# Attention on one core: dividing outputs instead of probabilities, and splitting a pair's heads through DRAM

## The chip, the cores and the metric

The kernel runs on one core of a Trainium2 chip. The time is that of one launch in device microseconds. Three runs are given for the kernel before.

## The reference

A decoder trunk of two layers works on 1040 tokens (16 learned meta tokens and 1024 real ones) with 1024 features. Layer 0 is a gated linear recurrence with a feed-forward block, layer 1 is causal attention with a forget gate and a feed-forward block. The change lies in the attention of layer 1, which has 16 heads of 64 features:

```
q = (x @ w_q) per head;  k, v = rmsnorm(h) @ kv_w per head;  c = cumsum(log_sigmoid(zf))
logits = q @ k.T * 64**-0.5 + (c[query] - c[key]),  causal
p = softmax(logits)
o = p @ v;   mix = o @ w_out
```

All arithmetic is float32 in the reference.

## The kernel before

Features lie on partitions and tokens along the free dimension. A float32 product is made of three matmuls on float32r parts: each operand is split into a high part (a rounding cast on ACT) and a low part (operand minus high part, a subtraction on DVE). `split` at line 98 (with the cast at line 97) does that for weights and for activations.

Heads are handled in pairs, eight pairs of 128 partitions. `project` (line 784) multiplies the normalised activations by the pair's weights for k, v or q in three token blocks (`BLK_A`, or `BLK_B` for q) and writes the product, times the normaliser r2, to a whole unit of SBUF: unit 17 for k, 18 for q, 16 for v (lines 798 and 800). `turn` (line 803) transposes v. `halves` (line 826) makes the operands of one head out of its 64 partitions of the pair's unit: the keys `ks` hold the high part on one half of the partitions and the low part on the other, and two query tiles `qs` hold high and low parts in both arrangements. That is four casts on ACT (lines 837, 841, 842, 844) and two subtractions on DVE (lines 838, 843) for each head and block. One matmul over 128 partitions then sums two products of parts. The tile `cn` holds the forget sums of the head, broadcast from DRAM (line 835).

The work is cut into 48 units: 16 heads by three groups of 342 queries. `score_steps` makes a unit's probabilities in three strips of 114 queries (QT): score matmuls (lines 879 to 882), an addition of c with a running minimum on DVE (line 884), the exponential with its sum on ACT (line 887), the reciprocal of the sum (line 888) and the multiplication of the whole strip by it on DVE (line 889). `sum_steps` transposes the strips on PE (line 909), splits the transposes into `pTh` on ACT (line 913) and `pTl` on DVE (line 914), sums over keys in one PSUM bank `po` (lines 921, 922), and adds the two halves of the bank to the head's output (line 933 on ACT, 934 on DVE), which is stored to DRAM `ob` (line 936). The last pair's outputs stay in SBUF.

PE's order is written out by hand. `scores_ahead` runs the sums of unit s beside the scores of unit s + 1 and calls `halves` for unit s + 2; `dense` is a second stream with the projections of pairs 1 to 7 and the first half of the output projection (`one`); `weave` mixes the two by their matmul columns. Pair 0 is projected before, in `heads0`. On the other engines and on SP's DMA queue, a scheduler orders instructions by readiness and priority; every queue runs in that order. The output projection loads the stored outputs in `oload` (line 990) into units that the projections' activations held, and splits them into `oh` and `ol`.

Of the kernel before, what the change touches and what calls it, by code (L numbers as in the profile page):

```python
# [8 lines left out]
F32 = mybir.dt.float32  # L9
F32R = mybir.dt.float32r  # L10
# [8 lines left out]
P = 128  # L19
# [36 lines left out]
def tile_yoco(ctx: ExitStack, tc: tile.TileContext, hT, gains, lbl, w_in, head_g, w_oa,  # L56
# [14 lines left out]
    def unit(i, name, dt=F32):  # L71
        return ar.tile([P, D if i in (30, 31) else T], dt, tag=f"u{i}", name=nm(name))
# [4 lines left out]
    def tmp(tag, n, dt=F32):  # L77
        return sm.tile([P, 358], dt, tag=tag, name=nm(tag), bufs=SMB[tag])[:, :n]

    def f(ap):  # L80
        return ap.bitcast(F32)
# [201 lines left out]
    h_dram = [nc.dram_tensor(f"h{j}", [KT, P, T], F32, kind="Internal").ap() for j in range(3)]  # L283
    o_dram = nc.dram_tensor("ob", [KT, P, T], F32, kind="Internal").ap()
    c_dram = nc.dram_tensor("csum", [BH, T], F32, kind="Internal").ap()


    hn = [(unit(kt, f"hnh{kt}", F32R), unit(8 + kt, f"hnl{kt}", F32R)) for kt in range(KT)]
# [470 lines left out]

    KS, QS, VS, CN = [24, 25], [(33, 34), (6, 7)], [[35, 36], [4, 5]], [12, 13]
    PU = [14, 15, 39, 44, 38, 19]
    NB = len(BLK_B)
# [5 lines left out]
    pair = [dict() for _ in range(KT)]  # L770
    head_ = [dict() for _ in range(2 * KT)]
    seen = set()
    count = {"p": 0, "pt": 0}

    def rot(key, slots):
# [8 lines left out]
    def project(which, hp, i):  # L784

        p = pair[hp]
        if which not in p:
            src, c0, g, u = {"k": (kv_w, 0, 8, 17), "v": (kv_w, D, 8, 16), "q": (w_q, 0, 4, 18)}[which]
            p[which] = (WA.cols(src, [c0 + hp * P], gsb[:, g]), unit(u, which))
        w, dst = p[which]  # L790
        t0, n = (BLK_B if which == "q" else BLK_A)[i]
        pt, sl = psum("pj")[:, :n], slice(t0, t0 + n)
        yield from mm3s(pt, [(w(kt), y[kt]) for kt in range(KT)], sl)
        while hp and which != "v" and ("split", 2 * hp - 1, i) not in seen:
            yield None
        with tc.high_priority(offset=OFF):
            if which == "q":
                V.scalar_tensor_tensor(dst[:, sl], pt, -HD ** -0.5, r2[:, sl], ALU.mult, ALU.mult)
            else:
                V.tensor_mul(dst[:, sl], pt, r2[:, sl])  # L800
        seen.add((which, hp, i))

    def turn(hp, i):

        p = pair[hp]
        if i == 0:
            p["vs"] = [unit(VS[hp % 2][j], f"vs{j}", F32R)[:, :D].rearrange("p (k c) -> p k c", c=P) for j in range(2)]
            p["tail"] = tmp("res", 2 * P, F32R).rearrange("p (k c) -> p k c", c=P)
        vT = p["v"][1]
        pt = psum("g")  # L810
        for j, (k0, kw) in enumerate(KEYS[3 * i:3 * i + 3]):
            PE.transpose(pt[:kw, j * P:(j + 1) * P], vT[:, k0:k0 + kw], ident)
        p3 = pt.rearrange("p (k c) -> p k c", c=HD)
        n = 3 - i // 2
        for j in range(2):
            parts = [(p["vs"][j][:QT, 3 * i:3 * i + n], p3[:QT, j:2 * n:2])]
            if i == 0:
                parts.append((p["vs"][j][96:, :1], p3[96:, j:j + 1]))
            elif i == 2:
                parts.append((p["tail"][:QT, j:j + 1], p3[:QT, 4 + j:5 + j]))  # L820
            for d, q in parts:
                A.copy(d[:, :, :HD], q)
                V.tensor_sub(d[:, :, HD:], q, f(d[:, :, :HD]))
        seen.add(("turn", hp, i))

    def halves(n, i):

        h = head_[n]
        if i == 0:
            h["k"] = unit(KS[n % 2], "ks", F32R)  # L830
            h["q"] = [unit(u, "qs", F32R) for u in QS[n % 2]]
            h["c"] = unit(CN[n % 2], "cn")
        a, b = (hi, lo) if n % 2 else (lo, hi)
        sl = slice(BLK_A[i][0], BLK_A[i][0] + BLK_A[i][1])
        nc.sync.dma_start(h["c"][:, sl], c_dram[n:n + 1, sl].to_broadcast([P, BLK_A[i][1]]))
        x, k = pair[n // 2]["k"][1], h["k"]
        A.copy(k[a, sl], x[a, sl])
        V.tensor_sub(k[b, sl], x[a, sl], f(k[a, sl]))
        sl = slice(BLK_B[i][0], BLK_B[i][0] + BLK_B[i][1])
        x, (q1, q2) = pair[n // 2]["q"][1], h["q"]  # L840
        A.copy(q1[a, sl], x[a, sl])
        A.copy(q2[b, sl], x[a, sl])
        V.tensor_sub(q2[a, sl], x[a, sl], f(q1[a, sl]))
        A.copy(q1[b, sl], f(q2[a, sl]))
        seen.add(("split", n, i))

    def dense():
        for hp in range(1, KT):
            for i in range(NB):
                yield from project("v", hp, i)  # L850
                if i:
                    turn(hp, i - 1)
                    yield 6 * P
            for i in range(NB):
                yield from project("k", hp, i)
                if i == 0:
                    turn(hp, 2)
                    yield 6 * P
                yield from project("q", hp, i)
        while ("split", 2 * KT - 1, NB - 1) not in seen:  # L860
            yield None
        yield from one()

    def score_steps(s):


        n, g = divmod(s, NB)
        h, g0 = head_[n], BLK_B[g][0]
        out = h[g] = []
        for i in range(3):  # L870
            q0 = g0 + i * QT
            kn = q0 + QT
            L = unit(rot("p", PU), "L")
            c4 = sm.tile([P, 8], F32, tag="c4", name=nm("c4"), bufs=4)[:QT]
            pcs = pieces(kn)
            for x, (a, b) in enumerate(pcs):
                pt = psum("pd")[:QT, :b - a]
                last = x == len(pcs) - 1
                PE.matmul(pt, h["q"][0][:, q0:q0 + QT], h["k"][:, a:b], start=True, stop=False)  # L879
                PE.matmul(pt, h["q"][1][:, q0:q0 + QT], h["k"][:, a:b], start=False, stop=not last)  # L880
                if last:
                    PE.matmul(pt[:, b - a - QT:], identb[:QT], maskb[:QT], start=False, stop=True)
                with tc.high_priority(offset=OFF):
                    V.tensor_tensor_reduce(L[:QT, a:b], pt, h["c"][:QT, a:b], 1.0, 3e38 if x == 0 else c4[:, x - 1:x],
                                           ALU.add, ALU.min, c4[:, x:x + 1])
                if last:
                    A.activation(L[:QT, :kn], L[:QT, :kn], AF.Exp, scale=-1.0, bias=c4[:, x:x + 1], accum_out=c4[:, 5:6])
                    V.reciprocal(c4[:, 6:7], c4[:, 5:6])
                    V.tensor_scalar(L[:QT, :kn], L[:QT, :kn], c4[:, 6:7], None, ALU.mult)  # L889
                    out.append((L, kn))  # L890
                yield 2 * (b - a) + last * QT

    def sum_steps(s):

        n, g = divmod(s, NB)
        g0, gn = BLK_B[g]
        pu = head_[n][g]
        p, j = pair[n // 2], n % 2
        nk = 3 * g + 3
        av = psum("po")  # L900
        pT = {}

        def turned(kt):
            c0 = rot("pt", [0, gn, 2 * gn])
            k0, kw = KEYS[kt]
            f0 = max(0, kt - 3 * g)
            pt = psum("g")
            for i in range(f0, 3):
                PE.transpose(pt[:kw, i * QT:(i + 1) * QT], pu[i][0][:QT, k0:k0 + kw], ident[:QT, :QT])  # L909
            ts = slice(f0 * QT, gn)  # L910
            th, tl = pTh[:kw, c0:c0 + gn], pTl[:kw, c0:c0 + gn]
            with tc.high_priority(offset=OFF):
                A.copy(th[:, ts], pt[:kw, ts])
                V.tensor_sub(tl[:, ts], pt[:kw, ts], f(th[:, ts]))  # L914
            pT[kt] = th, tl, ts
            return 2 * (gn - f0 * QT)

        def summed(kt):
            th, tl, ts = pT[kt]
            v = (p["vs"][j][:, kt] if kt < 8 else p["tail"][:, j])[:th.shape[0]]  # L920
            PE.matmul(av[:, ts], v, th[:, ts], start=(kt == 0), stop=False)  # L921
            PE.matmul(av[:, ts], v, tl[:, ts], start=False, stop=(kt == nk - 1))  # L922
            return 2 * (gn - ts.start)

        for kt in range(nk + AHEAD):
            if kt < nk:
                yield turned(kt)
            if kt >= AHEAD:
                yield summed(kt - AHEAD)
        r, r_ = (hi, lo) if j else (lo, hi)  # L930
        hp, sl = n // 2, slice(g0, g0 + gn)
        ot = o_last[0][:, sl] if hp == KT - 1 else tmp("sq", gn)
        A.copy(ot[r], av[r, :gn])
        V.tensor_add(ot[r], ot[r], av[r_, :gn])
        if hp < KT - 1:
            nc.sync.dma_start(o_dram[hp][r, sl], ot[r])

    def scores_ahead():

# [136 lines left out]
```

## Time and profile before

| | |
|---|---|
| median of three runs | 2875.55 us (2873.24 to 2882.78) |
| profiled execution, its time | 2883.05 us |
| its span | 2881.1 us |
| mean granted TensorE clock | 0.982 |
| busy share: PE, PEld, DVE, ACT, POOL | 96%, 94%, 64%, 44%, 13% |
| share of the DMA engines' span, hardware queue | 19.2% |

PE is the matmul engine and PEld its weight loads, DVE is VectorE, ACT ScalarE, POOL GpSimd, SP the engine that issues the DMAs. A line L889 is line 889 of the kernel before. The span runs from the first to the last instruction. A granted clock of 1.00 is 2.4 GHz and 0.50 is 1.2 GHz; a value between is a mean over both. In rows of waits, the engine and line on the left stood still until the one on the right was done.

### The profile page before, as it was taken

Reading aid. Unit: us, or ns where it says so; the run is one execution under the profiler, and the core shown is the slowest. Engines: PE = TensorE matmul, PEld = TensorE weight load, DVE = VectorE, ACT = ScalarE, POOL = GpSimd, SP = SyncE. Lnnn points to the kernel's source line nnn. Section 1 sums busy time; section 2 is a strip of 40 time slices with the busy share of each in tenths; the row PEclk is TensorE's granted clock in tenths of the full one; section 3 lists DMA queues with packets and bytes.
Section 4 is the critical chain, followed back from the end, with each engine's and each line's share of the span. In section 5 each row is a group of like instructions: output and inputs, shape, how many; then the busy total and the mean of one; then the engine's idle time right before and its main releaser. Section 6 shows DMA issues by size and latency. Waiting matters only on the chain. (4 is left out here: it accounts for less than half of the span.)

```text
span 2881.1 us, 45581 instructions
## 1 busy us (share of the span) xinstructions
PE 2768.6 (96%) x17706; PEld 2709.2 (94%) x17706; DVE 1830.8 (64%) x3737; ACT 1258.2 (44%) x2421; POOL 369.6 (13%) x741
## 2 busy tenths in 40 slices
PE   8999999989999999999889999999989999999997
PEld 8999999989999999999789988898989999999997
DVE  5545445285655655566878888887684665565566
ACT  6445445455322322233566666666555232232232
POOL 2000000041100000004400000000240100010012
PEclk9999999999999999999899999999999999999999
DMA  4111111142211111112311111112242111121103
GB/s 132 30 38 30 38 40 49 37 125 62 66 38 52 45 52 38 44 52 67 92 45 45 45 45 45 45 45 93 70 124 59 45 52 52 30 65 39 52 30 113
DMA packets 202921, 163.14 MB, mean 57 GB/s; under 512 B 13984, under 2 KB 194128, under 8 KB 202704
## 3 DMA queue, kind: packets, MB, share of 16 engines
q1 hardware_dynamic: 202704, 160.23, 19.2%
q8 instruction: 138, 2.26, 0.3%
q14 instruction: 79, 0.65, 0.1%
HBM read 139.53 MB, written 20.66 MB: 56 GB/s over the span
## 5 line engine op out<-in xcount | busy, mean ns | idle before, releaser
L145 PE MATMUL pj<-x,wh 128*128 128x342 f32 (+1 forms) x2640 | 871.1, 330 | 12.6 <-DVE u L607 6.3
L149 PE MATMUL pj<-x,wl 128*128 128x342 f32 (+1 forms) x2640 | 849.3, 322 | 2.8 <-DVE wl L98 2.8
L148 PE MATMUL pj<-x,wh 128*128 128x342 f32 (+1 forms) x2640 | 849.3, 322 | 0.0
L145 PEld LDWEIGHTS pj<-x,wh 128*128 128x128 f32 x2640 | 500.8, 190 | 18.9 <-DVE u L607 7.2
L149 PEld LDWEIGHTS pj<-x,wl 128*128 128x128 f32 x2640 | 499.9, 189 | 3.1 <-DVE wl L98 3.1
L148 PEld LDWEIGHTS pj<-x,wh 128*128 128x128 f32 x2640 | 501.5, 190 | 0.1
L145 PE MATMUL g<-h,wh 128*128 128x342 f32 (+1 forms) x1056 | 339.0, 323 | 0.3
L149 PE MATMUL g<-h,wl 128*128 128x342 f32 (+1 forms) x1056 | 337.7, 321 | 0.4 <-DVE wl L138 0.4
L148 PE MATMUL g<-h,wh 128*128 128x342 f32 (+1 forms) x1008 | 323.8, 322 | 0.0
L97 ACT CAST wh<-raw 128x1024 fp32r<-128x1024 f32 x142 | 146.0, 1045 | 341.6 <-PE g L148 282.1
L145 PE MATMUL pj<-hnh,wh 128*128 128x356 f32 (+1 forms) x720 | 261.8, 364 | 9.3 <-ACT wh L97 7.0
L681 DVE TENSOR_TENSOR acc<-acc,g 128x342 f32<-128x342 f32 (+1 forms) x288 | 147.2, 511 | 193.6 <-PE g L149 193.4
L98 DVE TENSOR_TENSOR wl<-raw,wh 128x1024 fp32r<-128x1024 f32 x142 | 180.6, 1281 | 87.1 <-ACT wh L97 76.3
L149 PE MATMUL pj<-hnh,wl 128*128 128x356 f32 (+1 forms) x720 | 233.1, 324 | 0.8 <-DVE wl L98 0.8
L148 PE MATMUL pj<-hnl,wh 128*128 128x356 f32 (+1 forms) x720 | 232.8, 323 | 0.0
L612 ACT ACTIVATE y<-u,cw 128x342 f32<-128x342 f32 (+1 forms) x258 | 150.5, 584 | 182.6 <-DVE u L607 171.9
L188 POOL TENSOR_TENSOR acc<-acc,sq 128x342 f32<-128x342 f32 (+1 forms) x162 | 168.9, 1049 | 426.5 <-ACT sq L187 396.4
L613 DVE SCALAR_TENSOR_TENSOR y<-u,cw,y 128x342 f32<-128x342 f32 (+1 forms) x258 | 148.5, 576 | 111.4 <-ACT y L612 111.2
L607 DVE TENSOR_TENSOR u<-pj,r 128x342 f32<-128x342 f32 (+1 forms) x258 | 132.2, 513 | 114.1 <-PE pj L149 110.8
L145 PEld LDWEIGHTS g<-h,wh 128*128 128x128 f32 x1056 | 198.7, 189 | 2.5 <-ACT h L97 0.6
L149 PEld LDWEIGHTS g<-h,wl 128*128 128x128 f32 x1056 | 199.4, 189 | 0.6 <-DVE wl L138 0.6
L148 PEld LDWEIGHTS g<-h,wh 128*128 128x128 f32 x1008 | 190.6, 189 | 0.7 <-DVE h L98 0.2
(237 smaller groups left out, 4937.8 us busy)
## 6 DMA issues: line engine op xcount, KB each, us to landing
raw<-in_w_up_dram SPq DMA_DIRECT2D x84, 512.0 KB, 4.0
raw<-in_w_dn_dram SPq DMA_DIRECT2D x42, 512.0 KB, 4.7
raw<-in_w_in_dram SPq DMA_DIRECT2D x32, 512.0 KB, 4.1
raw<-in_kv_w_dram SPq DMA_DIRECT2D x16, 512.0 KB, 4.1
res<-h SPq DMA_DIRECT2D x44, 171.0 KB, 2.8
h<-mix SPq DMA_DIRECT2D x40, 171.0 KB, 2.2
cn<-csum SPq DMA_DIRECT2D x32, 171.0 KB, 3.6
raw<-in_w_oa_dram SPq DMA_DIRECT2D x8, 512.0 KB, 3.5
```

What stands on the lines that cost most here:

```text
L97: A.copy(hi, src)
L98: V.tensor_sub(lo, src, f(hi))
L145: PE.matmul(pt, wh, xh[:, sl], start=(j == 0), stop=False)
L148: PE.matmul(pt, wh, xl[:, sl], start=False, stop=False)
L149: PE.matmul(pt, wl, xh[:, sl], start=False, stop=(j == n - 1))
L188: eng.tensor_add(acc, acc, sq)
L607: V.tensor_mul(u[:, 2:], pt, r()[:, sl])
L612: A.activation(y, u[:, 2:], AF.Copy, scale=cw[:, j, 2:3])
L613: V.scalar_tensor_tensor(y, u[:, 1:n + 1], cw[:, j, 1:2], y, ALU.mult, ALU.add)
L681: V.tensor_add(acc_u[ot][:, sl], acc_u[ot][:, sl], pt)
```

## The change

1. The probabilities are no longer divided by their sums. The reciprocals of a unit's three strips go to a small tile `rg` and by a DMA of 4-byte pieces to DRAM (`rsum`). At the beginning of the unit's sums they are loaded again, broadcast over 64 partitions, into `rr` (tag `rstd`), and the output is multiplied by them.
2. A unit's output is put together in another way: two copies on ACT out of `po` (lines 955, 956), an addition and a multiplication on POOL (lines 957, 958). For the last pair the addition stays on DVE, and a multiplication is added there (lines 951, 952).
3. The store of an output to `ob` is issued at the beginning of the next unit's sums, behind the load of its `rr`.
4. k and q of a pair are split as a whole, one cast and one subtraction over 128 partitions for each block, into two units (17, 18) that all pairs share. Both parts are stored to DRAM (`kq`), and `halves` loads a head's partitions into both halves of its tiles: two loads for the keys and four for the queries for each block.
5. The dense stream projects k, then q, then v of a pair, where it projected v and then k and q in turn. It does not wait any more for the previous pair's heads to be split. The v transposes of a block come behind the projection that follows.

```diff
+    r_dram = nc.dram_tensor("rsum", [BH, T], F32, kind="Internal").ap()
+    kq_dram = nc.dram_tensor("kq", [2, KT, 2, P, T], F32, kind="Internal").ap()
...
         if which not in p:
-            src, c0, g, u = {"k": (kv_w, 0, 8, 17), "v": (kv_w, D, 8, 16), "q": (w_q, 0, 4, 18)}[which]
-            p[which] = (WA.cols(src, [c0 + hp * P], gsb[:, g]), unit(u, which))
+            src, c0, g = {"k": (kv_w, 0, 8), "v": (kv_w, D, 8), "q": (w_q, 0, 4)}[which]
+            p[which] = (WA.cols(src, [c0 + hp * P], gsb[:, g]), unit(16, "v") if which == "v" else kq_dram["kq".index(which), hp])
...
-        while hp and which != "v" and ("split", 2 * hp - 1, i) not in seen:
-            yield None
         with tc.high_priority(offset=OFF):
-            if which == "q":
-                V.scalar_tensor_tensor(dst[:, sl], pt, -HD ** -0.5, r2[:, sl], ALU.mult, ALU.mult)
+            if which == "v":
+                V.tensor_mul(dst[:, sl], pt, r2[:, sl])
             else:
-                V.tensor_mul(dst[:, sl], pt, r2[:, sl])
+                if not kq_parts:
+                    kq_parts.extend(unit(u, "kq", F32R) for u in (17, 18))
+                x, xh, xl = tmp("u", n), *(u[:, sl] for u in kq_parts)
+                if which == "q":
+                    V.scalar_tensor_tensor(x, pt, -HD ** -0.5, r2[:, sl], ALU.mult, ALU.mult)
+                else:
+                    V.tensor_mul(x, pt, r2[:, sl])
+                split(xh, xl, x)
+                for j, part in enumerate((xh, xl)):
+                    nc.sync.dma_start(dst[j][:, sl], f(part))
...
-        a, b = (hi, lo) if n % 2 else (lo, hi)
+        r = (lo, hi)[n % 2]
         sl = slice(BLK_A[i][0], BLK_A[i][0] + BLK_A[i][1])
+        for j, rows in enumerate((lo, hi)):
+            nc.sync.dma_start(f(h["k"][rows, sl]), kq_dram[0, n // 2, j][r, sl])
         nc.sync.dma_start(h["c"][:, sl], c_dram[n:n + 1, sl].to_broadcast([P, BLK_A[i][1]]))
-        x, k = pair[n // 2]["k"][1], h["k"]
-        A.copy(k[a, sl], x[a, sl])
-        V.tensor_sub(k[b, sl], x[a, sl], f(k[a, sl]))
         sl = slice(BLK_B[i][0], BLK_B[i][0] + BLK_B[i][1])
-        x, (q1, q2) = pair[n // 2]["q"][1], h["q"]
-        A.copy(q1[a, sl], x[a, sl])
-        A.copy(q2[b, sl], x[a, sl])
-        V.tensor_sub(q2[a, sl], x[a, sl], f(q1[a, sl]))
-        A.copy(q1[b, sl], f(q2[a, sl]))
+        for x, q in enumerate(h["q"]):
+            for j, rows in enumerate((lo, hi)):
+                nc.sync.dma_start(f(q[rows, sl]), kq_dram[1, n // 2, j ^ x][r, sl])
...
     def dense():
+        todo = []
         for hp in range(1, KT):
-            for i in range(NB):
-                yield from project("v", hp, i)
-                if i:
-                    turn(hp, i - 1)
-                    yield 6 * P
-            for i in range(NB):
-                yield from project("k", hp, i)
-                if i == 0:
-                    turn(hp, 2)
-                    yield 6 * P
-                yield from project("q", hp, i)
+            for which in "kqv":
+                for i in range(NB):
+                    yield from project(which, hp, i)
+                    if todo:
+                        turn(*todo.pop())
+                        yield 6 * P
+                    if which == "v":
+                        todo.append((hp, i))
+        turn(*todo.pop())
...
-                    V.reciprocal(c4[:, 6:7], c4[:, 5:6])
-                    V.tensor_scalar(L[:QT, :kn], L[:QT, :kn], c4[:, 6:7], None, ALU.mult)
+                    V.reciprocal(rg[:, i:i + 1], c4[:, 5:6])
+                    if i == 2:
+                        nc.sync.dma_start(r_dram[n, g0:g0 + 3 * QT].rearrange("(i q) -> q i", q=QT), rg)
...
+        rr = tmp("rstd", gn)
+        rows = r if hp == KT - 1 else lo
+        nc.sync.dma_start(rr[rows], r_dram[n:n + 1, sl].to_broadcast([HD, gn]))
+        for dst, src in stores:
+            nc.sync.dma_start(dst, src)
+        stores.clear()
...
-        ot = o_last[0][:, sl] if hp == KT - 1 else tmp("sq", gn)
-        A.copy(ot[r], av[r, :gn])
-        V.tensor_add(ot[r], ot[r], av[r_, :gn])
-        if hp < KT - 1:
-            nc.sync.dma_start(o_dram[hp][r, sl], ot[r])
+        if hp == KT - 1:
+            ot = o_last[0][:, sl]
+            A.copy(ot[r], av[r, :gn])
+            V.tensor_add(ot[r], ot[r], av[r_, :gn])
+            V.tensor_mul(ot[r], ot[r], rr[r])
+        else:
+            ot, o2 = tmp("sq", gn)[lo], tmp("sq2", gn)[lo]
+            A.copy(ot, av[lo, :gn])
+            A.copy(o2, av[hi, :gn])
+            G.tensor_add(ot, ot, o2)
+            G.tensor_mul(ot, ot, rr[lo])
+            stores.append((o_dram[hp][r, sl], ot))
```

How the instructions move is shown at two places. The first is DVE in the loop's regular part, before the change (an ISA row is the addition with minimum and the read of its result):

```order
L888 RECIPROCAL c_2116_15539<-c_2116_15539 114x1
L843 TENSOR_TENSOR qs_15613<-q_15467,qs_15612 64x342
L889 TENSOR_SCALAR L_15538<-L_15538,c_2116_15539 114x584
L888 RECIPROCAL c_2123_15570<-c_2123_15570 114x1
L889 TENSOR_SCALAR L_15569<-L_15569,c_2123_15570 114x698
L934 TENSOR_TENSOR sq_15595<-sq_15595,po_15518 64x342
L800 TENSOR_TENSOR k_15331<-pj_15545,r_829_6125 128x342
L914 TENSOR_TENSOR pTl_13244<-g_15623,pTh_13243 128x342
L884 ISA L_15634,c_2135_15635<-pd_15636,cn_15161 114x406
L884 ISA c_2135_15635 114x1
L838 TENSOR_TENSOR ks_15611<-k_15331,ks_15611 64x342
```

And DVE in the regular part with the change:

```order
L893 ISA L_15540,c_2151_15541<-pd_15542,cn_15301 114x356
L893 ISA c_2151_15541 114x1
L807 SCALAR_TENSOR_TENSOR u_15563<-pj_15462,r_829_6125 128x342
L897 RECIPROCAL rg_15492<-c_2151_15541 114x1
L932 TENSOR_TENSOR pTl_13274<-g_15555,pTh_13273 114x342
L98 TENSOR_TENSOR kq_12767<-u_15563,kq_12766 128x342
L932 TENSOR_TENSOR pTl_13274<-g_15573,pTh_13273 114x342
```

Between the subtractions for `pTl` there is no multiplication of a strip, no head's subtraction and no output addition; one subtraction for the pair's block (L98) has come.

The second place is SP's DMA queue, before the change, over some two and a half heads' units:

```order
L936 DMA ob<-sq_14266 64x342
L835 DMA cn_14740<-csum 128x356
L835 DMA cn_14740<-csum 128x342 x2
L936 DMA ob<-sq_14431 64x342
L115 DMA raw_15324<-in_kv_w_dram 128x8x128
L936 DMA ob<-sq_14621 64x342
L936 DMA ob<-sq_14721 64x342
L835 DMA cn_15161<-csum 128x356
```

With the change, in a part of one unit, where a second head of a pair is loaded:

```order
L848 DMA ks_15298<-kq 64x356 x2
L849 DMA cn_15301<-csum 128x356
L853 DMA qs_15299<-kq 64x342
L899 DMA rsum<-rg_14858 114x3x1
L853 DMA qs_15300<-kq 64x342 x2
L848 DMA ks_15298<-kq 64x342 x2
L849 DMA cn_15301<-csum 128x342
L916 DMA rstd_15000<-rsum 64x342
L918 DMA ob<-sq_14974 64x342
```

The loads of a head's parts, the store and the load of the reciprocals and the store of an output of the unit before share the queue, and the head's loads stand around the reciprocals' store.

## Rows read from the trace of the kernel before

**Rows 1.** The page, busy us of each engine (share of the span) and instructions.

```profile
PE 2768.6 (96%) x17706; PEld 2709.2 (94%) x17706; DVE 1830.8 (64%) x3737; ACT 1258.2 (44%) x2421; POOL 369.6 (13%) x741
```

**Rows 2.** Stretches: busy us of PE, PEld, DVE, ACT, POOL; clock, DMA share, GB/s.

```profile
1345.00:1470.00 125.00, 103.21 (x571) 96.61 (x570) 98.61 (x201) 69.68 (x152) 48.92 (x41) 0.85 0.31 91
1470.00:1950.00 480.00, 459.42 (x3101) 434.01 (x3100) 406.39 (x1143) 302.90 (x756) 32.26 (x17) 0.99 0.16 44
1950.00:1980.00 30.00, 22.98 (x124) 19.67 (x123) 25.40 (x51) 23.94 (x48) 0.00 (x0) 0.78 0.55 170
1980.00:2080.00 100.00, 99.42 (x668) 97.14 (x668) 62.04 (x159) 55.81 (x122) 8.85 (x10) 1.00 0.17 54
1740.00:1750.00 10.00, 7.40 (x36) 6.21 (x36) 8.72 (x19) 5.16 (x14) 1.90 (x1) 0.83 0.11 33
1890.00:1900.00 10.00, 8.42 (x45) 7.83 (x44) 7.23 (x15) 6.44 (x15) 1.78 (x1) 0.83 0.20 59
```

**Rows 3.** Waits of PE, 1470 to 1950 us: total us, times, longest us.

```profile
PE po L922 <- DVE pTl L914: 10.6, 15, 2.2
PE g L909 <- DVE pTl L914: 2.7, 4, 0.9
PE g L909 <- DVE L L889: 1.7, 2, 0.9
PE po L921 <- ACT pTh L913: 1.6, 4, 0.7
```

**Rows 4.** Groups by line on DVE, 1470 to 1950 us: busy us, mean ns, idle before.

```profile
L889 DVE TENSOR_SCALAR L<-L,c 114x698 f32<-114x698 f32 (+8 forms) x119 | 75.6, 638 | 2.6
...
L838 DVE TENSOR_TENSOR ks<-k,ks 64x342 fp32r<-64x342 f32 (+1 forms) x38 | 23.0, 605 | 2.3 <-ACT ks L837 1.1
L934 DVE TENSOR_TENSOR sq<-sq,po 64x342 f32<-64x342 f32 x40 | 20.4, 510 | 12.6 <-ACT sq L933 11.7
L843 DVE TENSOR_TENSOR qs<-q,qs 64x342 fp32r<-64x342 f32 x37 | 18.7, 505 | 2.5 <-ACT qs L841 1.9
...
L798 DVE SCALAR_TENSOR_TENSOR q<-pj,r 128x342 f32<-128x342 f32 x20 | 10.2, 509 | 3.0 <-PE pj L149 2.2 <-PE po L921 0.6
```

**Rows 5.** Line 98's subtractions over 128 partitions: ns min/median/max, first and last start.

```profile
L98 DVE TENSOR_TENSOR x<-acc,x x24: 499/516/1248, 1350.1 to 1420.8; 128x342 fp32r<-128x342 f32 x16, 128x356 fp32r<-128x356 f32 x8
```

**Rows 6.** Groups by line on ACT, 1470 to 1950 us.

```profile
L837 ACT CAST ks<-k 64x342 fp32r<-64x342 f32 (+1 forms) x38 | 18.2, 479 | 4.9 <-DVE k L800 4.7
...
L844 ACT CAST qs<-qs 64x342 fp32r<-64x342 f32 x37 | 17.6, 476 | 1.4 <-DVE qs L843 0.5
L933 ACT COPY sq<-po 64x342 f32<-64x342 f32 x40 | 17.5, 437 | 7.8 <-PE po L922 7.3
```

**Rows 7.** Timeline from 1738 us (start, us); durations of line 188, ns min/median/max.

```profile
1741.82 1.90 POOL L126 TENSOR_TENSOR raw<-raw,gsb 128x1024 f32<-128x1024 f32 x1 [36.31 <-DVE c L884]
1741.88 2.21 DVE L838 TENSOR_TENSOR ks<-k,ks 64x342 fp32r<-64x342 f32 x1
...
L188 POOL TENSOR_TENSOR acc<-acc,sq x162: 904/952/1902, 11.6 to 2865.2; 128x342 f32<-128x342 f32 x131, 128x356 f32<-128x356 f32 x31
```

**Rows 8.** DMA issues, 1470 to 1950 us: KB each, median us to landing.

```profile
cn<-csum SPq DMA_DIRECT2D x26, 171.0 KB, 3.7
ob<-sq SPq DMA_DIRECT2D x40, 85.5 KB, 2.0
```

**Rows 9.** Timeline of SP's issues from 1500 us (start, us).

```profile
1506.03 0.45 SPq L936 DMA_DIRECT2D ob<-sq  x1
```

**Rows 10.** 1950 to 1980 us: the longest wait of PE, and an ACT group.

```profile
PE pj L148 <- DVE ol L98: 3.3, 2, 2.7
L844 ACT CAST qs<-qs 64x342 fp32r<-64x342 f32 x5 | 2.4, 476 | 0.1
```

**Rows 11.** Waits of PE, 1345 to 1470 us.

```profile
PE pj L145 <- DVE z L743: 4.6, 2, 4.2
...
PE g L909 <- DVE L L889: 2.7, 3, 1.4
```

More of the change, by code (lines that the diff above doesn't have):

```diff
@@ L772, in tile_yoco @@
     seen = set()
+    kq_parts, stores = [], []
     count = {"p": 0, "pt": 0}
@@ L869, in score_steps @@
         out = h[g] = []
+        rg = sm.tile([P, 3], F32, tag="rg", name=nm("rg"), bufs=2)[:QT]
         for i in range(3):
@@ L901, in sum_steps @@
         pT = {}
+        hp, sl = n // 2, slice(g0, g0 + gn)
+        r, r_ = (hi, lo) if j else (lo, hi)
+        rr = tmp("rstd", gn)
[4 more added lines that the diff above has]
+        stores.clear()
         def turned(kt):
@@ L929, in sum_steps @@
                 yield summed(kt - AHEAD)
-        r, r_ = (hi, lo) if j else (lo, hi)
-        hp, sl = n // 2, slice(g0, g0 + gn)
-        ot = o_last[0][:, sl] if hp == KT - 1 else tmp("sq", gn)
-        A.copy(ot[r], av[r, :gn])
-        V.tensor_add(ot[r], ot[r], av[r_, :gn])
-        if hp < KT - 1:
-            nc.sync.dma_start(o_dram[hp][r, sl], ot[r])
+        if hp == KT - 1:
[10 more added lines that the diff above has]
+            stores.append((o_dram[hp][r, sl], ot))
     def scores_ahead():
```

## The prediction, made before the changed kernel was run

> **What bounds the kernel now.** I read the page's busy times first: TensorE (PE) works 96% of the span, VectorE (DVE) 64%, ScalarE (ACT) 44% [rows 1]. A change that takes work from DVE and ACT can give back only the time in which PE stands still or runs at the low clock, so I looked for that time, stage by stage [rows 2]. The edited code runs from 1345 us (first projections of pair 0) to 2080 us. From 1470 to 1950 us the loop of 48 units is in its regular part: PE is busy 459.42 of 480 us, so it idles 20.6 us, while DVE is busy 406.39 us (85%) and ACT 302.90 us (63%). From 1980 to 2080 us PE does the same mixture, with the output projection as its dense work and no head to be split any more: DVE 62%, ACT 56%, and PE idles 0.58 us in 100. From 1950 to 1980 us PE idles 7.0 us of 30, from 1345 to 1470 us 21.8 of 125, and the granted clock is 0.78 and 0.85 there; in two 10 us windows of the regular part it is 0.83 [rows 2].
>
> The waits say on whom PE stood: in the regular part the three longest rows, together 15.0 us, name DVE: the low half of a transposed probability (pTl, L914) comes late, or the scaled probabilities of L889 do [rows 3]. No wait names a DMA. The chain behind each wait is: transposes on PE, cast on ACT, subtraction on DVE, sum on PE. It is late because DVE takes its instructions in order and other work stands in front.
>
> **What the change removes from DVE and ACT** in the 480 us. L889 goes: 119 instructions, 75.6 us. The head splits go: L838, 23.0 us, and L843, 18.7 us. The last addition of the output, L934, 20.4 us, moves to POOL [rows 4]. That is 137.7 us. What comes: one subtraction for each k or q block of a pair, 40 in this stretch (the queries' row counts 20, and k has as many) [rows 4], 0.516 us each for 128x342 [rows 5]: 20.6 us. DVE goes from 406 to 289 us, 60%. L889 also stood in the chain from scores to transposes, which now starts right behind the exponential. On ACT four groups of casts go (37 or 38 each; the first and the last are shown): 4 x 18.0 = 72 us; 40 casts of 0.476 us come (19 us), and a second copy of the output, 40 x 0.437 = 17.5 us [rows 6]. ACT goes from 303 to 267 us, 56%.
>
> **What that is worth.** 60% and 56% are the loads of 1980 to 2080 us, where PE idles 0.58% [rows 2]; for 480 us that is 2.8 us. The regular part has weight splits, v transposes and POOL work besides, so I take twice that, 5.6 us: 20.6 - 5.6 = 15.0 us gained. The two windows at 0.83 lost 1.7 us of full-speed work each; without the long waits ahead of them they go: 3.4 us. **Regular part: -18.4 us** (bounds: 0, and -24 if all of it went).
>
> At the end, 1950 to 1980 us, ACT is busy 23.94 and DVE 25.40 of 30 us [rows 2], because the splits of the last two heads meet those of the output projection; PE waits 3.3 us for ol alone, and four groups of head casts stand among ACT's work, of which one is shown with 2.4 us [rows 10]. They become DMAs. In exchange v is projected last now, so that two of its transposes with their casts fall here, and the four loads of earlier outputs still wait for the last projection. I take **-3 us** (+3 to -9). At the start PE waited 4.6 us for z and 2.7 us for L889 [rows 11]. One DVE subtraction of two goes with each half split; against it stands a round trip through DRAM that is hardly covered there (next paragraph). I take **0** (+6 to -7). The multiplication added for the last pair (six on DVE, 0.51 us each, like L934 [rows 4]) lies behind the output projection's filler and costs nothing; without that filler it would be 3 us.
>
> **What it adds.** *Round trip of k and q.* DVE product 0.51, cast 0.48, subtraction 0.52 [rows 4 to 6], two stores at 0.45 us of SP each [rows 9] and 2.0 us to landing like ob, six loads at 0.45 and 3.7 us like cn [rows 8]: 10.8 us (5 to 20 with a queue in front). Between the last matmul of a pair's q block and the first score that reads it the new order has at least 183 matmuls; the regular part makes 3101 in 459 us, 0.148 us each [rows 2], so 27 us. A second head's loads have 271 or more, 40 us. So it is hidden, with 16 us to spare. Only block 2 of pair 0 has 79 matmuls, 11.7 us: 1 us to spare, hence the bound at the start. *SP.* 480 more DMAs in 48 units, 60 for each pair; 20 q blocks in 480 us [rows 4] make a pair 72 us, and 60 issues at 0.45 us take 27 of them [rows 9], so SP is not full. It takes them in order, and a store that waits for DVE holds those behind it; the order puts stores and sums behind events of the same unit, so I count microseconds, inside the 16. The longest block, a second head's 24 loads, is 11 us. *DMA volume.* 5.7 MB more per pair, some 79 GB/s above the 44 there; 170 GB/s is reached from 1950 to 1980 us at a share of 0.55 [rows 2]. *Sums.* Their round trip has 4-byte pieces, of which no row shows a price; it is bounded by ob's 2.0 us below and, allowing for double the slowest row shown, by 7.4 us above [rows 8]. Even the upper value is under a unit's 12 us (40 of L934 in 480 us [rows 4]), and nobody but POOL waits for it. *POOL.* An addition and a multiplication for each of 40 units, 0.95 us each like L188 [rows 7]: 76 us, with 32 us there now [rows 2], so POOL has time. ACT's second copy waits for the addition of the unit before; it was made a unit earlier. The output's store comes one unit later; the first reader is the output projection, so that costs nothing until the last stores of pair 6.
>
> **POOL and DVE.** At 1741.82 us POOL starts a 1.90 us multiplication, and the DVE subtraction that starts beside it takes 2.21 us [rows 7], where L843 of the same size takes 0.505 on the mean [rows 4]; PE idles 2.6 us in that window and drops in clock [rows 2]. So new POOL work could cost DVE as much as it takes off it; that is the second rival. The Trainium skill ("SBUF — State Buffer", section "SBUF: two separate sides") says that the two engines hold one port pair exclusively for a whole instruction, but of DVE's instructions only those in a two-port mode or with two SBUF inputs; by that rule 59 instructions remain at risk (40 subtractions and 19 weight splits), and the sum stays as above, where a lock for all would make it the rival's.
>
> **Sum.** -18.4 - 3 + 0 = -21 us. It is made against the profiled execution, 2883.05 us (span 2881.1 us), and gives 2862. That execution is 7.5 us above the median of three runs, 2875.55 us (2873.24 to 2882.78), and nothing shows whether the 7.5 us lie in the waits that I remove. With all of them there, the median would come to 2862, with none to 2854.5; I take the middle, **2858 us**. About 0.3%, 8.6 us, is what a measurement of this kernel tells from no change: faster means under 2867, slower over 2884.
>
> **Rivals.**
> *The waits change their engine* (0.10). Two thirds of DVE's stalls vanish only if the cast on ACT is in time, and ACT still runs the exponentials ahead of it. If half of the 15.0 us comes back as waits for pTh, with half the clock loss and half of the end: -11 us, and 2868 by the same middle. For it: the fourth row, 1.6 us, names ACT already [rows 3]. Against it: the stretch at 56%.
> *POOL blocks DVE* (0.08). If each of these instructions delayed DVE by its length, the 76 us would put DVE at 365 of 480 us, 76%. Between 62% (0.58% idle) and 85% (4.3%) [rows 2] that is 2.9%, 14 us of idle: 7 us gained, 8 with half the clock loss, 11 with the end, and 2868 by the same middle. For it: the 2.21 us. Against it: DVE reads PSUM in most of what is left, and rows of that kind (L934, mean 510 ns) [rows 4] show no such stretch.
> *The round trip is late* (0.08; slower). If SP stands behind a waiting store for longer than the 16 us to spare, each first head's score matmul waits on a DMA. At 3 us beyond, in 14 heads, that is +42 us over the forecast: 2900. It decides from a trip of 27 us on. For it: one queue, in order. Against it: 10.8 us, and no such wait now.
>
> **How the numbers follow.** Forecast 0.74, with a range of its own from 2842 (the median less 24 and 9) to 2866 (the profiled time less 15, the regular part without the clock, and 2). Rivals 0.10, 0.08, 0.08. Faster: 0.74 and some third of the first two rivals, 0.79; slower: 0.06 of the last; the rest, 0.15, within 0.3%. The range reaches from the forecast's low end, 2842, over the two rivals near 2868, to 2871; it leaves out the late round trip and the extremes.
>
> **What would show it.** Right: from the start of the loop to its end L889, L838, L843 gone, DVE near 60%, ACT near 56%, PE idle of 3 to 8 us in the regular part at clock 1.00, no wait of PE on ks, qs or cn. Wrong: PE waits that name a DMA of kq (third rival), POOL beside long DVE subtractions (second), or pTh L931 in place of pTl L932 (first). If DVE falls to 60% and PE still idles 15 us, the idle was never queueing on DVE, and the first step of the sum is wrong.

## The result, and the profile after

The changed kernel takes **3023.99 us** (median of four runs, 3020.86 to 3026.25), the kernel before 2879.11 us beside it: 1.0505 of the time, 95% interval 1.049 to 1.0521. It is 145 us slower, where 2858 us was forecast and no time above 2871 us was in the range. Of all the runs in this document one, of the kernel with the later transpose below, took 3026 us at a granted clock of 0.84 and is left out of its figures.

The page of the changed kernel, busy times and the hardware DMA queue (packets, MB, share of 16 engines' span):

```profile
PE 2789.3 (92%) x17706; PEld 2730.4 (90%) x17706; DVE 1713.8 (57%) x3509; ACT 1211.1 (40%) x2319; POOL 451.1 (15%) x825
q1 hardware_dynamic: 260112, 206.78, 28.3%
```

DVE and ACT lost the work that they were meant to lose [rows 1], and PE's share fell all the same. The stretch of the regular part, columns as in [rows 2]:

```profile
1470.00:1950.00 480.00, 384.20 (x2441) 363.09 (x2441) 241.35 (x743) 213.30 (x536) 90.86 (x78) 0.90 0.54 98
```

In the same 480 us PE makes 2441 matmuls in place of 3101, at a clock of 0.90 in place of 0.99. DVE is busy 50% of it and ACT 44%: no engine is full. The DMA engines are busy 54% of the time, more than three times as much as before, and move 98 GB/s, 2.2 times as much. The reciprocals, three a unit, mark the loop's begin and end. Line 888 of the kernel before, then line 897 of the changed one (ns min/median/max, first and last start):

```profile
L888 DVE RECIPROCAL c<-c x144: 142/162/167, 1458.9 to 2033.8; 114x1 f32<-114x1 f32 x144
```

```profile
L897 DVE RECIPROCAL rg<-c x144: 142/164/166, 1454.1 to 2178.8; 114x1 f32<-114x1 f32 x144
```

The last one comes 145.0 us later than before: the whole loss lies in the loop. The waits there, 1470 to 1950 us, of PE, SP's queue and DVE in turn (total us, times, longest us):

```profile
PE pd L888 <- DVE c L893: 67.4, 15, 18.9
...
SPq L916 <- DMA rsum<-rg: 147.2, 27, 7.8
SPq L853 <- DMA kq<-kq: 49.7, 15, 8.2
...
DVE rg L897 <- DMA rsum<-rg: 58.4, 15, 9.0
```

PE still waits for DVE [rows 3], for longer and in another place. But DVE itself stands now, and on a transfer: its reciprocal (L897) waits until the store of reciprocals has left the one of rg's two buffers that it is to write. SP waits on that store too, with the load (L916) that reads what has just been stored.

One unit shows how it hangs together. SP's issues from 1697 us (start, us); then the same 16 us, 1697 to 1713, in 40 slices of 0.4 us (busy tenths of the DMA engines, and GB/s); then one instruction each of DVE and PE with the idle time before it:

```profile
1697.66 0.43 SPq L899 DMA_DIRECT2D rsum<-rg  x1
1698.19 0.39 SPq L812 DMA_DIRECT2D kq<-kq  x1
1698.63 0.42 SPq L115 DMA_DIRECT2D raw<-in_kv_w_dram  x1
1699.10 0.67 SPq L812 DMA_DIRECT2D kq<-kq  x1
1707.49 0.45 SPq L916 DMA_DIRECT2D rstd<-rsum  x1
...
DMA  5555789965214969499929762798678755623545
GB/s 86 168 147 133 125 254 189 27 13 6 31 20 85 55 28 50 23 31 33 49 13 32 42 42 51 140 232 244 207 199 255 226 106 157 157 86 34 192 133 120
...
1707.44 0.22 DVE L897 RECIPROCAL rg<-c 114x1 f32<-114x1 f32 x2 [4.38 <-DMA rsum<-rg]
...
1708.26 0.43 PE L940 MATMUL po<-pTl,vs 114*128 114x342 f32 x1 [3.00 <-DVE pTl L932]
```

SP issues the small store, two stores of k or q and half a megabyte of weights within 1.5 us. From 1699.8 us on the DMA engines are busy some 60% of the time and move almost nothing, some 35 GB/s, until the small store is done near 1707; then the queued bytes go at over 200 GB/s. Meanwhile SP stands at L916 and DVE at L897, with the subtraction for which PE waits queued behind it.

### The profile page after: what moved, and what is told of

Read it like the earlier page. It is cut to its first block, busy times and chain, and to the rows that moved or that the text cites. A ratio compares the mean times of both kernels' runs of the same rounds, so it can differ in the third digit from the quotient of the medians.

```text
span 3024.6 us, 46285 instructions
## 1 busy us (share of the span) xinstructions
PE 2789.3 (92%) x17706; PEld 2730.4 (90%) x17706; DVE 1713.8 (57%) x3509; ACT 1211.1 (40%) x2319; POOL 451.1 (15%) x825
## 5 line engine op out<-in xcount | busy, mean ns | idle before, releaser
L98 DVE TENSOR_TENSOR wl<-raw,wh 128x1024 fp32r<-128x1024 f32 x142 | 181.8, 1290 | 101.4 <-ACT wh L97 86.4
```

What stands on the lines that cost most here:

```text
L98: V.tensor_sub(lo, src, f(hi))
```

## The experiments

The theory from this profile: **A**, SP's queue stands in order at the load behind each fresh store, and everything behind it is late. Its rivals: **B**, the transfers themselves are slow while the small pieces are written; **C**, rg has too few buffers; **D**, the round trip of k and q.

**The load one unit's sums later.** In `sum_steps`:

```diff
-        nc.sync.dma_start(rr[rows], r_dram[n:n + 1, sl].to_broadcast([HD, gn]))
-        for dst, src in stores:
-            nc.sync.dma_start(dst, src)
...
                 yield summed(kt - AHEAD)
+        nc.sync.dma_start(rr[rows], r_dram[n:n + 1, sl].to_broadcast([HD, gn]))
+        for dst, src in stores:
+            nc.sync.dma_start(dst, src)
```

> The same instructions and the same transfers as the changed kernel; only the load of a unit's reciprocals (L916) and the output store of the unit before stand at the end of the unit's sums in the program and not ahead of them, so that the small store (L899) has most of a unit to land before SP comes to the load. Theory A (SP's queue in order stands at L916 until that store has landed, 238 us in all, everything behind it is late): SP's waits at L916 fall below 40 us, DVE's waits for rsum below 10 us, the time comes to 2865-2905 us. Theory B (the DMA engines are loaded too much, share 0.54 with many small pieces, so that all transfers land late): the transfers are the same, the time stays above 2980 us. Theory C (DVE stands because rg has only two buffers): the store is issued at the same place, so the time stays above 2980 us unless SP is what delays the store, which is A.

2991.8 us (1.0391, 1.037 to 1.0412). This told nothing on A: the scheduler that orders the program put every instruction of the loop where it had been, on every engine and in SP's queue, so it is the changed kernel once more, its twin. That it was 32 us faster came up again in the last runs.

**Without division.** The store, the load and the multiplications are left out:

```diff
-                    if i == 2:
-                        nc.sync.dma_start(r_dram[n, g0:g0 + 3 * QT].rearrange("(i q) -> q i", q=QT), rg)
...
-        nc.sync.dma_start(rr[rows], r_dram[n:n + 1, sl].to_broadcast([HD, gn]))
...
-            G.tensor_mul(ot, ot, rr[lo])
```

> Leaves the division out: neither the store nor the load of the reciprocals, no multiplication by them; k and q still go through DRAM, the output stores stay one unit later. Theory A: without L916 SP has only the waits of the k and q loads on their own stores (L853 and L848, 85 us); 2855-2890 us. Theory B: the transfers of k and q, the larger part of the volume, remain with a DMA share near 0.45; the time stays above 2950 us. Theory D (the round trip of k and q is late by itself): PE waits on ks or qs, above 2900 us.

2846.46 us in one run, below the range of every theory. B in its form "too many bytes" and D fall: k and q still go through DRAM at 130 GB/s, and no wait of PE names them.

**k and q alone.** As above, with the probabilities multiplied on DVE as before:

```diff
+                    V.tensor_scalar(L[:QT, :kn], L[:QT, :kn], c4[:, 6:7], None, ALU.mult)
```

> k and q split through DRAM as in the change, but the probabilities are multiplied by the reciprocals on DVE as in the kernel before (120 us of DVE in all) and nothing of the sums goes through DRAM. Theory A: SP is free of L916; DVE has about 365 of 480 us; 2865-2900 us. Theory B: above 2950 us. Theory D: PE waits on ks or qs, above 2900 us.

2861.25 us, 0.9944 of before (0.9929 to 0.9959), faster than any theory had it: this half of the change is a gain of 0.6% by itself.

**Pieces of 12 bytes.**

```diff
-  r_dram[n, g0:g0 + 3 * QT].rearrange("(i q) -> q i", q=QT)
+  r_dram[n, g0:g0 + 3 * QT].rearrange("(q i) -> q i", i=3)
```

> The reciprocals are stored as 114 pieces of 12 bytes in place of 342 of 4 bytes; the load is the same, so that the divisors reach other columns (only their order is changed). Theory A with the pieces as what makes the landing long: the wait at L916 falls from about 8 us to 3-5 us a unit, 2900-2970 us. Theory A with a fixed cost of a store and load in sequence: the landing stays above 6 us and the time above 2990 us. Theory B: 10% fewer packets by number, little less load; above 2990 us.

2860.79 us in one run, below every range; the reciprocals reach other columns here, so it does not compute the reference's result. The same 1.3 KB in the same number of DMAs, in 114 pieces and not 342: 131 us less than the twin, which ran beside it (2991.8), and 163 less than the changed kernel, which ran in another sitting (on another occasion). From the trace's records of landings (medians over the loop) the store took 8.1 us before this edit and 3.2 us with it.

**The sums alone**, in the kernel before, with the 4-byte pieces:

> The kernel before with the output division alone: sums through DRAM by 4-byte pieces, outputs added and multiplied on POOL, stores one unit later, heads split on DVE and ACT as before. SP has 144 issues fewer than half of the change's here and little stands behind the load. If the 4-byte pieces cost by what queues behind them, this is far less slow than the change: 2870-2910 us. If DVE's wait for the two buffers of rg is what costs, or the pieces cost by themselves: 2960-3020 us.

2869.78 us, 0.9967 (0.9955 to 0.9979), just under the lower of its ranges. SP waits here for the store even longer than in the changed kernel, 1470 to 1950 us:

```profile
SPq L911 <- DMA rsum<-rg: 188.3, 40, 8.3
```

and the kernel is still faster than before. The store lands as late as in the change or nearly so, 6.9 us (median) against 8.1. What differs is how much is queued behind it: 54 GB/s in that stretch, against 98. So neither half is slow; together they are.

**The load elsewhere.** The 4-byte store stays, the load reads another tensor and waits for no fresh store; the division is left out:

```diff
-  nc.sync.dma_start(rr[rows], r_dram[n:n + 1, sl].to_broadcast([HD, gn]))
+  nc.sync.dma_start(rr[rows], c_dram[n:n + 1, sl].to_broadcast([HD, gn]))
```

> The 4-byte store stays, but the load of L916 reads a row of csum in place of rsum, so that it waits for no store (the outputs are multiplied by other numbers than the reciprocals; the division is left out). Same transfers by number and size. Theory A (SP's queue stands at L916 until the store has landed, and all behind it is late): 2860-2900 us, few waits on rsum. Theory B (the 342 pieces occupy the DMA engines that they are on for 6-8 us, and every other transfer with packets behind them lands late): SP does not stand at L916 any more, but the loads and stores of k, q and the weights still land after up to 10-12 us; above 2940 us.

2961.7 us in one run. SP's wait for the store's landing is gone from L916 (its largest row is now at L853, loads of q behind their own stores: 78.6 us, 49.7 in the change), and most of the loss is still there: A is a part, B the larger one. The stretch 1470 to 1950 us:

```profile
1470.00:1950.00 480.00, 412.99 (x2726) 391.96 (x2726) 270.60 (x822) 237.33 (x599) 99.82 (x86) 0.94 0.59 109
```

**Three stores of 114 pieces of 4 bytes**, one for each strip:

```diff
-                    if i == 2:
-                        nc.sync.dma_start(r_dram[n, g0:g0 + 3 * QT].rearrange("(i q) -> q i", q=QT), rg)
+                    nc.sync.dma_start(r_dram[n, q0:q0 + QT].rearrange("(i q) -> q i", q=QT), rg[:, i:i + 1])
```

> The reciprocals of each strip are stored by a DMA of their own as soon as they are there: three stores of 114 pieces of 4 bytes a unit in place of one of 342; pieces and bytes in all as in the change, 96 DMAs more for SP. If the landing is priced by the piece (0.14 us for each on its engine, from 8.1 us for 342 and 3.2 us for 114 of 12 bytes), each lands in about 3 us, and what counts is the sum of pieces: theory B gives 2960-3030 us. Theory A gives 2880-2930 us, because the last store has landed sooner when SP comes to the load.

3222.73 us in one run, far above every range. So the price isn't by the piece: a store of 114 pieces of 4 bytes lands after 8.7 us (median), no sooner than one of 342, and three of them a unit lose 362 us against the kernel with 12-byte pieces, where the change and its twin lose 131 to 163 with as many pieces. What the strip's store and the unit's store share is that neighbouring pieces lie 4 bytes apart, 114 of them in 456 bytes. With 12 bytes a piece only 38 lie in as many.

**The same pieces, spread.** Against the run that loads elsewhere, the 4-byte pieces lie 64 bytes apart (and 16 in a second kernel, with 4 in place of 16 below):

```diff
-  r_dram = nc.dram_tensor("rsum", [BH, T], F32, kind="Internal").ap()
+  r_dram = nc.dram_tensor("rsum", [BH, T, 16], F32, kind="Internal").ap()
...
-  r_dram[n, g0:g0 + 3 * QT].rearrange("(i q) -> q i", q=QT)
+  r_dram[n, g0:g0 + 3 * QT, 0].rearrange("(i q) -> q i", q=QT)
```

> Like the run that loads elsewhere (2962 us; the division is left out there and here), and the same 342 pieces of 4 bytes a store, but in DRAM each piece lies 64 bytes from the next in place of 4, so that no two of them are neighbours. Theory B1 (the stall of all transfers after a store comes from small writes that fall next to each other: 342 words in 1368 bytes): the stall goes; 2845-2870 us. Theory B2 (it comes from the size or number of the pieces): 342 pieces of 4 bytes remain, 2940-2985 us.

> As the runs with the load elsewhere (pieces 4 bytes apart, 2962 us) and spread over 64 bytes (2859 us), division left out as there, but the 342 pieces of 4 bytes lie 16 bytes apart in DRAM. If the stall after a store grows with the number of pieces that fall close together, a quarter of it is left, some 1.5 us a store as with the 12-byte pieces: 2858-2880 us. If pieces that share any short stretch of DRAM stall in full: 2940-2975 us.

2858.98 us at 64 bytes and 2864.59 us at 16, one run each; the store lands after 2.7 and 3.5 us (medians). The loss of B is gone with as many pieces, as small, in as many DMAs. The regular part with 64 bytes, columns as above:

```profile
1470.00:1950.00 480.00, 458.74 (x3154) 438.49 (x3154) 317.44 (x963) 278.09 (x703) 111.71 (x98) 1.00 0.52 135
```

The same three issues behind a small store as shown above (kq, weights, kq), and the 16 us from 1708 us in 40 slices, with the pieces 64 bytes apart:

```profile
1708.55 0.43 SPq L899 DMA_DIRECT2D rsum<-rg  x1
1709.02 0.44 SPq L812 DMA_DIRECT2D kq<-kq  x1
1709.84 0.38 SPq L115 DMA_DIRECT2D raw<-in_kv_w_dram  x1
1710.32 0.53 SPq L812 DMA_DIRECT2D kq<-kq  x1
...
DMA  5654793265599999876225334364644998554163
GB/s 127 137 171 123 113 339 89 19 47 50 140 324 348 362 373 380 175 188 161 99 79 140 96 123 116 113 164 103 207 135 85 145 222 147 178 86 92 48 157 106
```

The queued bytes, the weights among them, begin to go through at 324 to 380 GB/s 4 us after the store's issue, where they did so only after nearly 10 us behind the 4-byte neighbours. The dip ahead of it, 19 to 50 GB/s for 1.2 us, does not show in the mean over all stores that follows.

Over all stores: in the record of DMA packets each store is a burst of small packets. Behind the 0.75 us in which the burst is densest I added up, microsecond by microsecond, the bytes of the packets of at least 512 bytes that start, and took the mean over the stores: 48 in each kernel, and of the strips' 144 the 104 whose bursts can be told apart (GB/s):

```
us behind the burst                    1    2    3    4    5    6    7    8
342 of 4 B, side by side (after)      91   49   31   29   25   25   38   95
the same, load elsewhere              88   49   55   47   47   52  113  178
114 of 4 B, side by side (strips)     95   38   36   36   43   46   49   73
114 of 12 B, side by side             89   50   83  152  164  152  143  121
342 of 4 B, 16 B apart                86   45  141  165  134  130  130  124
342 of 4 B, 64 B apart               109  107  140  135  123  132  115  116
```

About five microseconds of near standstill for everything that the core transfers, 48 times, then a backlog; with three times or four times as much room for a piece about one; with 16 times none.

**A mend with the reference's result.** The 12-byte pieces, and the multiplication reads the reciprocals with a stride of three:

```diff
-            G.tensor_mul(ot, ot, rr[lo])
+            G.tensor_mul(ot.rearrange("p (i q) -> p i q", q=QT), ot.rearrange("p (i q) -> p i q", q=QT),
+                         rr[lo].rearrange("p (q i) -> p i q", i=3))
```

> The store in 114 pieces of 12 bytes, and the multiplication reads the loaded reciprocals with a stride of three elements, so that each column gets its own: what is computed is the reference's. Both theories: the landing is 3 us, as in the run with the pieces alone; 2855-2866 us; a slower strided read on POOL would show in its multiplication (0.95 us now) and cost nothing.

2865.53 us, 0.9946 (0.9929 to 0.9962): 0.5% faster than the kernel before, and far faster than the changed one. Its regular part:

```profile
1470.00:1950.00 480.00, 460.81 (x3156) 439.78 (x3154) 316.48 (x963) 277.43 (x701) 114.61 (x98) 1.00 0.54 132
```

**Rows made on PE.** The reciprocals are transposed and stored as three rows of 456 bytes, first right behind the last reciprocal, then (second kernel) after the unit's third transposed tile, from `sum_steps`, where the load of the reciprocals and the stores of outputs also stand behind the unit's sums. The first kernel's lines:

```diff
+  gt, rw = psum("g"), tmp("y", QT)[:3]
+  PE.transpose(gt[:3, :QT], rg, ident[:QT, :QT])
+  A.copy(rw, gt[:3, :QT])
+  nc.sync.dma_start(r_dram[n, g0:g0 + 3 * QT].rearrange("(i q) -> i q", q=QT), rw)
```

> The reciprocals of a unit are transposed on PE (114x3 to 3x114), copied by ACT, and stored as three rows of 456 bytes; load, multiplication and all else as in the change; what is computed is the reference's. B1 and B2 alike: no small piece remains, no stall; the store lands in 2.0 to 2.3 us like ob's. It adds 48 transposes (about 0.1 us each, 5 us of PE) and 48 ACT copies of some 0.2 us. From the run without division (2846 us): 2850-2862 us. If PE stands at the transposes because the reciprocals come late: 2865-2890 us.

2998.25 us (1.0417, 1.0396 to 1.0439). Neither the gain nor the mishap of that size was expected. PE, which takes its work in order, stood at the transpose until DVE had the reciprocal:

```profile
PE g L900 <- DVE rg L897: 70.5, 33, 2.6
```

> As the run that turns the reciprocals on PE and stores three rows, but the transpose stands after the third probability tile of the unit's sums in place of right behind the last reciprocal, and the load of the reciprocals behind the sums; what is computed is the reference's. If PE's 88.8 us of waits for the reciprocals, with the clock that they cost, were all that was wrong with that run: 2850-2862 us, PE's wait at the transpose under 5 us. If the three-row store costs by itself: above 2870 us.

2867 us (median of four runs), 0.9964 (0.9948 to 0.998), 5 us above the expected range; the longest row of PE's waits in the stretch is 4.7 us. The transposes and the three-row store cost little, then. The first kernel is 131 us slower; its PE stands 100.6 us at the transposes over the whole run, 48 times some 2 us, and its granted clock in the stretch is 0.93, against 1.00 here. The two differ in the place of the load as well, so the split of the 131 us is not shown.

**On one chip.** The changed kernel, the one with the load at the end and the one that loads elsewhere once more, side by side:

> The changed kernel again, beside the next two on one chip. The run with the load at the end has the same order of instructions on every engine and took 2992 us in another sitting, the changed kernel 3024. If the difference is the sitting's or the chip's: both within 10 us of each other here. If it is in the program (where its buffers lie): 3015-3030 against 2985-3000 again.

> As said for the changed kernel beside it: within 10 us of it if the sitting made the difference, 25 to 40 us faster if the program does.

> The load that waits for no fresh store, on the same chip as the changed kernel: the difference between the two is what SP's wait for the store's landing costs. From the earlier figures 30 (against 2992) to 62 us (against 3024) faster than the changed kernel beside it; 2950-2975 us.

2998.88, 2995.75 and 2961.44 us (two runs each; before 2879.23). The changed kernel and its twin agree, so the 32 us lie in the chip or the sitting (the twin took 2992 us on one chip and 2996 on another); the kernel before differs by under 0.3% between sittings. SP's wait for the fresh store is worth 37 us, the difference of the first and the last, while that store lands late. With 12-byte pieces, 3.2 us to landing, the load still stands behind its store, and 2861 us lies between the 2859 and 2865 us of the spread pieces, where it does not.

So, from 2999 us: 37 us for SP standing at L916 (2961), 102 us for the standstill that the neighbouring pieces cause (2859), 13 us for the rest of the division, its small store, its load and its multiplications (2846); 2859 and 2846 are one run each. The kernel before is at 2878.

## Why the prediction was wrong

**The step that failed** is the one on the sums: "4-byte pieces, of which no row shows a price; it is bounded by ob's 2.0 us below and [...] by 7.4 us above [...]. Even the upper value is under a unit's 12 us, and nobody but POOL waits for it." The landing took 8.1 us, just above the upper bound. The size was the smaller error; what hangs on it was the larger. Three parties waited besides POOL: every other transfer of the core, SP, and DVE. For 7.4 us the step should have asked, as the prediction did for the trip of k and q, who stands in the same queue. A price with no row was bounded as a latency only; it was a price on a resource that all transfers share, and the row behind the lower bound, ob with pieces of 1368 bytes, is no relative of 342 single words. The Trainium skill ("DMA: Bandwidth & Descriptors", section "Specifications") says that transfers under 512 bytes are done by reading, modifying and writing. By that alone the pieces 64 bytes apart would cost as much as those side by side; the runs put 102 us between them.

**SP, "not full".** 27 of 72 us for the issues left out what SP waits for. The order shown ahead of the prediction has the load of the reciprocals a few rows behind their store, so SP stands there for the landing: 147 us in 480. A store that should have gone out when its reciprocals were ready then went out late: the one at 1697.66 us holds reciprocals of 1675 to 1678 us, and the reciprocal at 1707.44 us two units on had to wait for it. That closes the ring through rg's two buffers (C): DVE's 58.4 us are a consequence, since with spread pieces, and with rg as it was, no such wait remains among the longest. Whether a third buffer would have kept the standstill from DVE and PE was not tried, so how much of the loss runs through this ring stays open.

**The third rival** had the sign and the queue ("SP stands behind a waiting store"), but not the place. In the regular part no wait of PE names k's and q's trip; in the whole changed kernel one does, 4.5 us (PE pd L889 <- DMA qs<-kq) before 1470 us, where the prediction saw 1 us to spare, and none with the mend. And 0.08 was too little for a queue in order with 480 more issues in it.

**What held once the store is mended.** With 12-byte pieces the kernel is at 2861 to 2866 us, where 2842 to 2866 was the forecast's own range. No wait of PE names a DMA of ks, qs or kq. The volume, 132 GB/s, does no harm. ACT is busy 277 us of 480 (forecast 267). DVE is busy 316 (forecast 289). About 11 us of that is a wrong sum: neighbouring instructions of DVE overlap at their ends, so the 137.7 us of the four lines can't be taken off its busy time; without them the trace of the kernel before leaves 279.4 us, not 268.7. Some 5 us are PE's higher pace, and the subtraction behind k and q takes 774 ns and not 516:

```profile
L98 DVE TENSOR_TENSOR kq<-u,kq 128x342 fp32r<-128x342 f32 x35 | 27.1, 774 | 4.2 <-ACT kq L97 3.9
```

With the multiplication on POOL left out it takes 649 ns, and 586 with DVE's own in its place. That fits the second rival, for this one kind of instruction (both operands in SBUF); L932, which reads PSUM, is at 452 ns with and without. It is 10 us of DVE in the stretch and was not tried by itself.

**The regular part, -18.4 us, was too large, and its first step does not hold.** With the mend DVE's load falls from 85% to 66%, and PE is still idle 19.2 us of the stretch (20.6 before), where the prediction wanted 3 to 8 us and had 15 us as its sign that "the idle was never queueing on DVE". PE's waits for pTl fell from 13.3 to 7.0 us; the wait for the strip's addition (PE pd L888 <- DVE c L893), 0.9 us before, is 10.3 us now. All the same 3156 matmuls were made in the 480 us, 55 more: at 0.148 us each 8 us. Without any division it is 59 more. So idle time by the busy column does not measure what the change gives back; that a matmul which is held up counts as busy would explain it, and no run shows it. That the total lies at the slow edge of the forecast's own range is in part luck. **The start**, forecast 0, gave some 4 us: the first reciprocal comes at 1454.7 us with the mend, 1458.9 before, in one execution of each. **The end** can't be compared in the same stretch, since all work has moved forward.

## What to carry to other kernels

A tiny store can cost more than a large one: how its pieces lie in DRAM decides, and the price is paid by all transfers behind it. Give each partition's piece room, or write whole rows, and ask of every operation without a row not only how long it takes but who shares its queue and its resource meanwhile. A load right behind the store that it reads stops the issuing queue for the landing; whether moving the line in the program moves it in the queue must be read from the order. And a transpose put right behind what it needs makes PE, which takes its work in order, wait 2 us at a time, 100.6 us in all here.

## What the runs showed that was not expected

- Behind a store of neighbouring 4-byte pieces, 114 in 456 bytes, all transfers of the core fall to some 25 to 50 GB/s for about 5 us; 342 pieces in three such rows take no longer than 114 in one (8.1 and 8.7 us to landing). It fits a price for pieces that share a short stretch of DRAM, written one after another there and side by side elsewhere: 4 bytes apart five microseconds, 12 or 16 about one, 64 none. How long such a stretch is, and where the writes queue, stays open.
- The changed kernel differs by 0.8% between sittings (3024 and 2999 us) where the kernel before differs by under 0.3%.
- Two halves that each gain, 0.9944 and 0.9967, lose 4 to 5% together: one brings the standstill, the other the traffic that it holds up. That the traffic makes the difference is argued from the GB/s; no run varied it alone.
